# An encoder block on one core: output projection, queries, keys and memory output computed by rows, with the norms' results turned through DRAM

## The chip, the cores and the metric

The kernel runs on one core of a Trainium2 chip. The metric is the device time of one execution in microseconds; the time of a kernel is the median of its runs. The profile shows one execution in detail. Its engines are PE (TensorE matmul), PEld (TensorE weight load), DVE (VectorE), ACT (ScalarE), POOL (GpSimd) and SP (SyncE).

## The reference

One layer of an encoder for 256 tokens of width 2048, all in float32. Cut to what matters:

```python
h = rms_norm(x, norm_g[0])
q, k, v, g, lr, u_f, u_h, u_s = split(h @ w_in)
y_a = gla_mixer(q, k, v, g, lr, ...)                       # gated linear attention
y_b = rms_norm(fnet_mixer(u_f), grp_norm_g[0])             # fft over 256 tokens and 4 groups of 128 channels, real part
y_c = rms_norm(hyena_mixer(u_h, ...), grp_norm_g[1])       # long convolutions
y_d = rms_norm(shortconv_mixer(u_s, ...), grp_norm_g[2])
x = x + concat([y_a, y_b, y_c, y_d]) @ w_out               # output projection, 2048 x 2048
x = x + cross_attention(rms_norm(x, norm_g[1]), rms_norm(mem, mem_norm_g), w_xq, w_xkv, w_xo)
x = x + swiglu(rms_norm(x, norm_g[2]), w_gate_up, w_down)  # 2048 x 11264, 5632 x 2048
return rms_norm(x, final_norm_g)
```

Cross-attention has 4 heads of 512 over 256 memory tokens; `w_xq` gives the queries, `w_xkv` keys and values, and `w_xo` projects the heads' outputs back ("memory output").

## The kernel before, in words

**Numbers.** Every large product is taken in three parts: each float32 operand is split into a high half `h` (ACT copies it to float32r) and a low rest `l` (DVE subtracts), and the product is `hh + hl + lh`. An operand slot is a tile of 128 x 512: the high halves of 256 tokens, then their low halves.

**Weights.** The host packs all weights in the order in which they are used, in slabs of 128 x 2048 (1 MB, sixteen blocks of 128 x 128). `Stream._half` (L77) loads a slab through SP's queue, and for each half of it (eight blocks) ACT casts `wh` (L104) and DVE subtracts `wl` (L105). `Stream.take` (L109) hands out the next blocks and keeps up to three halves made ahead. Four halves are live until w_xo is nearly done, then three.

**Two forms of product.** By columns (`mm`, L304, called by `gemm`, L323): the weight block stays in the array and the activations stream. Per block there are two matmuls, `wh` against all 512 columns of the slot (L311) and `wl` against the 256 high ones (L312). The result is a block of 128 features x 256 tokens in two halves, which `merge` (L316) adds: ACT copies one out of PSUM, DVE adds. With `narrow` the first matmul is cut in two of 256 (L308, L309) that add up in PSUM, and no merge is needed. By rows (`gemm_rows`, L361, with `part_rows`, L353): the activations of 128 tokens stay and four weight blocks stream as 512 columns. For each half of the tokens there are three matmuls of 512 (L356, L357, L358). The result is 128 tokens x 512 features.

**Order of the work.** In `mixers` (L425): keys by columns (the first eight column blocks side by side, since memory's slots arrive one after the other), values by rows, then `w_in` in the order hyena, GLA's v by rows, GLA's q and k, three blocks of the short convolution, FNet narrow, the rest of the short convolution, GLA's gate. `out_proj` (L598) multiplies the four mixers' results, the first four column blocks in three parts, each behind one mixer. `attention` (L615) computes the queries of a head by columns, and each head's scores, softmax and values beside the next head's queries. `gate_up` (L757) and `down` (L834) work by rows.

**Between the products.** After w_out and w_xo a block of 128 features x 256 tokens is merged, added to the residual `x` (kept turned, features on partitions, in `res`), scaled by the norm's gain and split into the slots of the next product (`residual`, L584, and `rest`, L592). Squares are summed over features in `acc`, and a matmul by a column of ones (`rstd_begin`, L237, L247) gives the sum for each token. The norm's factor for each token is applied later, to the results. `rstd_end` (L291) spreads a factor over the partitions by a matmul with a diagonal matrix. `turn` (L813) takes the residual back to rows during gate_up: DVE transposes 32 x 32 pieces (L820), POOL stores them to DRAM (L823) and loads rows (L827). The hidden layer takes the same way: transposed by DVE (L776), stored (L779), loaded (L791) and split.

**Background work.** Everything small is a generator. `Background.poll` (called in every step of a product) advances those that are due by a clock that counts PE's and DVE's time as the author estimates it, and `drain` runs one to its end where its result is needed. The order in which the instructions then stand on each engine is laid out by the framework, which can put a later matmul ahead of one whose operands it takes to be late; `keep_place` (L219) holds some at their place.

Of the kernel before, what the change touches and what calls it, by code (L numbers as in the profile page):

```python
# [38 lines left out]
ROWS = ((256, 512), (704, 768), (NBLK - 48 * FT, NBLK))  # L39
# [86 lines left out]
class Background:  # L126
# [9 lines left out]
    def add(self, g):  # L136
        self.q.append([g, self.now])
        return g
# [29 lines left out]
class Block:  # L168
# [49 lines left out]

    def keep_place(self, mark):  # L219

        ins = self.nc.cur_bb.bb.instructions
        for n in range(mark, len(ins)):
            for j in range(n - 1, -1, -1):
                if ins[j].engine == ins[n].engine:
                    self.tc.add_manual_dep(ins[n], ins[j].name, mybir.DependencyInfo(
                        mybir.DependencyClass.NoSync, mybir.DependencyReason.DATA), reason="order")
                    break

    def sumsq(self, acc, src, first):
        if first:  # L230
            self.nc.scalar.activation(acc, src, AF.Square)
        else:
            s = self.tmp()
            self.nc.scalar.activation(s, src, AF.Square)
            self.tt(acc, acc, s, ALU.add)
# [33 lines left out]
    def rstd_bank(self, y, g=0, whole=False):  # L269

        nc = self.nc
        if whole:
            dg = self.dgp.tile([P, R], F32R, name="dgh", tag="dgh", bufs=2).bitcast(F32)
            self.bg.dve(256, 2)
            for r in range(2):
                s = slice(r * P, (r + 1) * P)
                nc.vector.tensor_scalar(out=dg[:, s], in0=self.ident, scalar1=y[:, 2 * g + r:2 * g + r + 1], scalar2=None, op0=ALU.mult)
            p = self.bank()
            nc.tensor.matmul(p[:, 0:R], self.ones, dg, start=True, stop=True)
            return p[:, 0:R]  # L280
# [5 lines left out]
        p = self.bank()  # L286
        for d in dg:
            nc.tensor.matmul(p[:, 0:R], self.onesr, d, start=d is dg[0], stop=d is dg[1])
        return p[:, 0:R]

    def rstd_end(self, y, g=0, keep=None, whole=False):  # L291
        rs = keep.tile([P, R], F32, name=f"krs{next(self.kept)}") if keep else self.rp.tile([P, R], F32, name="rs", tag="rs")
        self.nc.scalar.copy(rs, self.rstd_bank(y, g, whole))
        return rs

    def rstd_later(self, acc, n, box, keep=None, wait=2):

        box["col"] = self.rstd_begin([[acc]], n, keep)
        for _ in range(wait):
            yield  # L300
        box["rs"] = self.rstd_end(box["col"], 0, keep)
# [51 lines left out]
    def part_rows(self, p, r, slot, wh, wl, start, stop):  # L353

        hi, lo = slot[:, r * P:(r + 1) * P], slot[:, R + r * P:R + (r + 1) * P]
        self.nc.tensor.matmul(p[:, :], hi, wh, start=start, stop=False)  # L356
        self.nc.tensor.matmul(p[:, :], hi, wl, start=False, stop=False)  # L357
        self.nc.tensor.matmul(p[:, :], lo, wh, start=False, stop=stop)  # L358
        self.bg.pe(0.687)

    def gemm_rows(self, w, cols, slots, done=None, parts=None, before=None):  # L361
# [3 lines left out]
        nk = len(slots)  # L365
        for part, ks in enumerate(parts or [range(nk)]):
            if before:
                before(part)
            for k in ks:
                for p, col in zip(ps, cols):  # L370
                    wh, wl = self.st.take(w, k, col, 4)
                    for r in range(2):
                        self.part_rows(p[r], r, slots[k], wh, wl, k == 0, k == nk - 1)
                if done:
                    done(k)
                self.bg.poll()
        return ps


    def run(self):  # L380
# [9 lines left out]
        self.acc = cp.tile([P, R], F32, name="acc")  # L390
        self.mg = cp.tile([P, 16], F32, name="mg")
        self.eps = cp.tile([P, 8], F32, name="eps")[:, 0:1]
        self.gap(cp, 224)

        self.kd = nc.dram_tensor("keys", (P, 16 * R), F32, kind="Internal").ap()
        self.xr = nc.dram_tensor("xrows", (R, D), F32, kind="Internal").ap()
# [18 lines left out]
        make_identity(nc, self.ident)  # L415
        with self.tc.tile_pool(name="wx", bufs=1) as st.extra:
# [8 lines left out]
    def mixers(self):  # L425
# [42 lines left out]
        def prepare(mid):  # L468
# [5 lines left out]
            self.rsm = self.rstd_end(self.rcm, 0, self.cp)  # L474
            self.bg.add(hy.filters())
            nc.sync.dma_start(gl.lrw, self.t["lrw"])
            yield from squares("x", c[1])
            col = self.rstd_cols(c[1][:, 0:2], D)

            while not rows:  # L480
                yield SOON
            self.rsx = self.rstd_end(col, 0, mid, True)

        UF, UH, US = 1568, 2080, 3616
        cols, cur = [], {}
        for j in range(4):
            cols += [US + 512 + j * P, US + 1024 + j * P, US + j * P]
# [15 lines left out]
        with tc.tile_pool(name="mid", bufs=1) as mid:  # L503
            self.dgp = mid
            gl = Gla(self, mid)
            with tc.tile_pool(name="hyp", bufs=1) as hyp, tc.tile_pool(name="k2", bufs=8) as k2:
# [6 lines left out]
                def ev_k(i, p):  # L513
                    if i == 8:
                        for k in range(0, KT, 4):
                            self.load_x(k, 4)
                    nc.gpsimd.dma_start(self.kd[:, i * R:(i + 1) * R], self.merge(p))

                self.gemm("w_xkv", [i * P for i in range(16)], h, ev_k, first=(8, [[k] for k in range(KT)]), before=start_m)
                for hd in range(4):  # L520
                    for r, p in enumerate(self.gemm_rows("w_xkv", [D + hd * 512], h, start_x if hd == 3 else rows.append)[0]):
                        for c in range(2):
                            v, o = self.tmp(), (2 * hd + r) * 512 + c * R
                            nc.scalar.activation(v, p[:, c * R:(c + 1) * R], AF.Copy, scale=self.rcm[:, r:r + 1])
                            nc.gpsimd.dma_start(self.vd[:, o:o + R], v)
                self.bg.drain()
# [10 lines left out]
                self.gemm("w_in", cols[0:NSC], h, ev_s, narrow=True)  # L537
                self.bg.drain()

            with tc.tile_pool(name="glp", bufs=1) as glp:  # L540
                gl.open(glp)
                fn = Fnet(self, glp)
# [918 lines left out]
```

## Time and profile before

| | |
|---|---|
| time, median of 3 runs | 1484.07 us (1484.03 to 1484.11) |
| the profiled execution | 1483.97 us, its span 1482.2 us |
| mean granted clock of TensorE | 0.998 |
| DVE, ACT, POOL busy | 64%, 52%, 10% |
| DMA, mean share of 16 engines' time of the weights' queue | 53.9% |
| read from HBM | 291.18 MB, 206 GB/s with what is written |

Stages in the trace, by the start of their first large matmul, in us of the span:

| stage | from | to |
|---|---|---|
| keys | 5 | 98 |
| values | 98 | 195 |
| w_in | 195 | 461 |
| w_out | 461 | 550 |
| w_xq (attention beside it) | 550 | 658 |
| w_xo | 658 | 754 |
| w_gate_up | 754 | 1234 |
| w_down | 1234 | 1482 |

How to read a row of a profile: "L311 PE MATMUL pg<-act,wh 128*128 128x512 f32 x1" is line 311, engine, operation, the tile written and those read, the shape, and the count; times are in us unless marked ns. In a table of groups the numbers behind the bar are the busy time in us, the mean ns of one instruction, and the idle time of the engine ahead of them with what ended it. In a timeline the first two numbers are start and duration. Matmuls overlap: one of 512 columns is busy for 0.39 us, while the next starts 0.23 us after it.

### The profile page before, as it was taken

The page shows a single profiled execution, that of the slowest core. Times are in us where ns is not written, and L with a number is a line of the kernel's source. Part 1 is how long each engine was busy: PE and PEld are TensorE (multiplying, and loading weights), DVE is VectorE, ACT ScalarE, POOL GpSimd, SP SyncE. Part 2 cuts the span into 40 slices and gives each one's busy share as a digit, 9 for nine tenths or more (in the row PEclk, how much of TensorE's full clock was granted, in tenths as well). Part 3 has the DMA queues.
Part 4 walks back from the last instruction along what each step waited for, and adds up shares of the span by engine and source line. Part 5 has one row for each costly group of instructions (what it writes and reads, how often), then busy time and mean ns, then how long its engine had stood idle before and what let it go on. Part 6 is the DMA issues. An engine that isn't in the chain of part 4 may idle for free.

```text
span 1482.2 us, 19837 instructions
## 1 busy us (share of the span) xinstructions
PE 1471.8 (99%) x7586; PEld 1254.9 (85%) x7586; DVE 942.1 (64%) x1379; ACT 766.3 (52%) x1147; POOL 150.1 (10%) x260
## 2 busy tenths in 40 slices
PE   9999999999999999999999999999999999999997
PEld 8888888899899888888888888888888888888886
DVE  6687768778677777877665554555554456544444
ACT  6566655458555656656544444444444445434344
POOL 0100100000000001200042411111110112000000
PEclk9999999999999999999999999999999999999999
DMA  9976554454446555544567756666666666555554
GB/s 359 353 250 209 203 195 162 169 184 144 167 155 220 196 188 199 197 166 160 184 198 252 242 210 215 220 222 227 211 207 212 222 224 228 186 191 194 199 198 143
DMA packets 56174, 306.11 MB, mean 207 GB/s; under 512 B 9197, under 2 KB 10510, under 8 KB 24464
## 3 DMA queue, kind: packets, MB, share of 16 engines
q1 hardware_dynamic: 45632, 281.11, 53.9%
q0 software_dynamic: 10016, 23.08, 4.9%
q8 instruction: 59, 0.97, 0.3%
q10 hardware_dynamic: 432, 0.66, 0.1%
q14 instruction: 35, 0.29, 0.1%
HBM read 291.18 MB, written 13.63 MB: 206 GB/s over the span
## 4 chain that ended last, share of the span: by engine, by line
PE 96%; ACT 1%; DVE 1%; issue 0%; DMA 0%; SPq 0%; ACTq 0%; DVEq 0%
PE pg L311 21%; PE pg L356 17%; PE pg L357 17%; PE pg L358 17%; PE pg L312 11%; PE pm L357 1%; PE pm L356 1%; PE pm L358 1%; PE pm L311 1%; PE pm L986 1%; PE pg L308 1%; PE pg L309 1%; PE pm L738 1%; PE pm L312 1%; PE pm L711 0%; ACT wh L104 0%
## 5 line engine op out<-in xcount | busy, mean ns | idle before, releaser
L105 DVE TENSOR_TENSOR wl<-raw,wh 128x1024 fp32r<-128x1024 f32 (+1 forms) x503 | 611.7, 1218 | 469.9 <-ACT wh L104 464.7
L104 ACT CAST wh<-raw 128x1024 fp32r<-128x1024 f32 (+1 forms) x503 | 523.7, 1042 | 577.9 <-PE pg L358 391.6
L311 PE MATMUL pg<-act,wh 128*128 128x512 f32 x1296 | 455.9, 394 | 0.2 <-DVE act L196 0.2
L312 PE MATMUL pg<-act,wl 128*128 128x256 f32 x1472 | 412.1, 280 | 0.0
L356 PE MATMUL pg<-wh,act 128*128 128x512 f32 x1008 | 393.1, 390 | 0.0
L358 PE MATMUL pg<-wh,act 128*128 128x512 f32 x1008 | 392.4, 389 | 0.0
L357 PE MATMUL pg<-wl,act 128*128 128x512 f32 x1008 | 392.3, 389 | 0.0
L311 PEld LDWEIGHTS pg<-act,wh 128*128 128x128 f32 x1296 | 243.3, 188 | 53.4 <-DVE act L196 0.5
L312 PEld LDWEIGHTS pg<-act,wl 128*128 128x128 f32 x1472 | 276.8, 188 | 1.1 <-issue 0.4
L356 PEld LDWEIGHTS pg<-wh,act 128*128 128x128 f32 x1008 | 189.2, 188 | 40.2 <-issue 0.4
L358 PEld LDWEIGHTS pg<-wh,act 128*128 128x128 f32 x1008 | 189.2, 188 | 39.8
L357 PEld LDWEIGHTS pg<-wl,act 128*128 128x128 f32 x1008 | 189.3, 188 | 39.1
L779 POOL DMA_DIRECT2D hidden<-u x88 | 57.1, 656 | 311.0 <-DVE u L776 309.5
L308 PE MATMUL pg<-act,wh 128*128 128x256 f32 x176 | 50.0, 284 | 0.0
L309 PE MATMUL pg<-act,wh 128*128 128x256 f32 x176 | 49.5, 281 | 0.0
L356 PE MATMUL pg<-wh,f 128*128 128x512 f32 x120 | 46.7, 389 | 0.0
L357 PE MATMUL pg<-wl,f 128*128 128x512 f32 x120 | 46.7, 389 | 0.0
L358 PE MATMUL pg<-wh,f 128*128 128x512 f32 x120 | 46.7, 389 | 0.0
L196 DVE TENSOR_TENSOR tmp<-pg,tmp 128x256 f32<-128x256 f32 x86 | 35.9, 418 | 8.5 <-ACT tmp L318 6.9
L823 POOL DMA_DIRECT2D xrows<-tmp x48 | 27.7, 586 | 129.1 <-DVE tmp L820 126.0
L318 ACT COPY tmp<-pg 128x256 f32<-128x256 f32 x85 | 31.0, 366 | 9.5 <-PE pg L312 8.7
L308 PEld LDWEIGHTS pg<-act,wh 128*128 128x128 f32 x176 | 33.3, 189 | 0.1
(285 smaller groups left out, 1252.8 us busy)
## 6 DMA issues: line engine op xcount, KB each, us to landing
raw<-in_W SPq DMA_DIRECT2D x246, 1024.0 KB, 4.9
raw<-in_W SPq DMA_DIRECT2D x11, 512.0 KB, 7.4
hidden<-u POOLq DMA_DIRECT2D x88, 64.0 KB, 3.1
tmp<-hidden POOLq DMA_DIRECT2D x44, 128.0 KB, 4.2
res<-in_xT SPq DMA_DIRECT2D x8, 512.0 KB, 6.0
k<-in_mem SPq DMA_DIRECT2D x8, 256.0 KB, 7.9
k<-in_x SPq DMA_DIRECT2D x8, 256.0 KB, 8.3
keys<-tmp POOLq DMA_DIRECT2D x16, 128.0 KB, 5.9
```

The lines of the kernel that those rows point to most:

```text
L104: nc.scalar.copy(wh[:, a:b], r[:, a:b])
L105: nc.vector.tensor_tensor(out=wl[:, a:b], in0=r[:, a:b], in1=wh[:, a:b].bitcast(F32), op=ALU.subtract)
L196: self.nc.vector.tensor_tensor(out=out, in0=a, in1=b, op=op)
L308: self.nc.tensor.matmul(p[:, 0:R], wh, slot[:, 0:R], start=start, stop=False)
L309: self.nc.tensor.matmul(p[:, 0:R], wh, slot[:, R:512], start=False, stop=False)
L311: self.nc.tensor.matmul(p[:, :], wh, slot[:, :], start=start, stop=False)
L312: self.nc.tensor.matmul(p[:, 0:R], wl, slot[:, 0:R], start=False, stop=stop)
L318: self.nc.scalar.copy(t, p[:, R:512])
L356: self.nc.tensor.matmul(p[:, :], hi, wh, start=start, stop=False)
L357: self.nc.tensor.matmul(p[:, :], hi, wl, start=False, stop=False)
L358: self.nc.tensor.matmul(p[:, :], lo, wh, start=False, stop=stop)
L779: nc.gpsimd.dma_start(to[:, :, 32 * a:32 * a + 32], u[32 * a:32 * a + 32, :].rearrange("f (b t) -> f b t", t=32))
```

## The change

- **By rows.** Keys (in groups of two, one and one of 512 columns), output projection, queries and memory output (two, one, one) and FNet's projection go from `gemm` to `gemm_rows`. The order of the packed weights follows (`ROWS` marks which halves lie at the rows' offset).
- **Residual by rows.** `x` is loaded by rows; a result of 128 tokens x 512 features is added to it as it is (`add_rows`), and its squares are summed by ACT along the row (`sq`, then `row_norm`). `acc`, its column sums by matmul and `turn` go.
- **Turned through DRAM.** What the next product needs with features on partitions (the scaled, split residual after w_out and w_xo, and the queries) is transposed by DVE in pieces of 32 x 32, stored by POOL in runs of 32 elements (`store_turned`, `turned`) and loaded back in tiles of 128 x 256 (`arrive`), which ACT and DVE split. For each block of 512 columns that is 4 transposes, 16 stores and 4 loads. Keys are stored in the same way.
- **Order of w_out.** Its first two column blocks run together, in the order hyena, GLA, short convolution, FNet (before: four column blocks of 128, hyena and short convolution, FNet, GLA).
- **FNet.** Projection by rows; the transform over tokens comes first, on sums and differences of the two halves of the tokens, then the one over channels; both in split halves (before: over channels first, in plain float32).
- **Norms' factors.** `rstd_end` becomes two steps with a pause between them; one in plain float32 (`whole`, L279) is now in split halves too. The squares of x are taken once the first values are under way.
- **Last column block.** The residual's columns 1536 to 2047 enter the last product's PSUM bank by four matmuls with the identity at the start of gate_up (before: eight transposes at the start of down).

The diff, cut to its core:

```diff
-ROWS = ((256, 512), (704, 768), (NBLK - 48 * FT, NBLK))
+ROWS = ((0, 512), (704, 768), (880, 944), (1152, NBLK))
...
+    def store_turned(self, to, u, src):
+        nc = self.nc
+        self.bg.dve(src.shape[1])
+        nc.vector.transpose(u, src)
+        to = to.rearrange("(b f) t -> f b t", f=32)
+        for a in range(4):
+            nc.gpsimd.dma_start(to[:, :, 32 * a:32 * a + 32],
+                                u[32 * a:32 * a + 32, :].rearrange("f (b t) -> f b t", t=32))
...
-                self.gemm("w_xkv", [i * P for i in range(16)], h, ev_k, first=(8, [[k] for k in range(KT)]), before=start_m)
+                for cols in ([0, 512], [1024], [1536]):
+                    first = dict(parts=[[k] for k in range(KT)], before=start_m) if len(cols) > 1 else {}
+                    for c, ps in zip(cols, self.gemm_rows("w_xkv", cols, h, **first)):
+                        for r in range(2):
+                            self.store_turned(self.kd[c:c + 512, r * P:(r + 1) * P], hy.piece(), ps[r][:, :])
...
-                self.gemm("w_in", [UF + i * P for i in range(4)], h, lambda i, p: nc.scalar.copy(fn.u[i], p[:, 0:R]), narrow=True)
+                fn.feed(self.gemm_rows("w_in", [UF], h)[0])
...
-                self.out_proj(lambda n: self.bg.drain((g_sc, g_fn, g_gla)[n]))
+                self.out_proj(lambda n: self.bg.drain((g_gla, g_sc, g_fn)[n]))
...
+    def turned(self, to, c, srcs):
+        for r, x in enumerate(srcs):
+            for j in range(0, 512, R):
+                self.store_turned(to[c * 512 + j:c * 512 + j + R, r * P:(r + 1) * P], self.tmp(), x[:, j:j + R])
+
+    def arrive(self, src, c, put, ok=None):
+        m = []
+        for k in range(4 * c, 4 * c + 4):
+            m.append(self.tmp())
+            self.nc.gpsimd.dma_start(m[-1], src[k * P:(k + 1) * P, :])
+        yield 9.0
+        while ok and not ok():
             yield SOON
+        for i, t in enumerate(m):
+            mark = self.mark()
+            put(4 * c + i, t)
+            self.keep_place(mark)
+            yield SOON
+
+    def add_rows(self, n, c, ps):
+        for r in range(2):
+            x = self.half(c, r)
+            self.tt(x, x, ps[r], ALU.add)
+        for r in range(2):
+            self.nc.scalar.activation(self.bank()[:, :], self.half(c, r), AF.Square, accum_out=self.sq[n][:, 4 * r + c:4 * r + c + 1])
+        self.turned(self.xf[n], c, [self.half(c, r) for r in range(2)])
...
-        self.gemm("w_out", [i * P for i in range(16)], slots,
-                  lambda i, p: self.residual(i, p, V_NG + 16 + i, h2[i] if i < 8 else None),
-                  first=(4, [list(range(8, 16)), list(range(4, 8)), list(range(0, 4))]), before=ready)
-        self.late = self.bg.add(self.rest(h2, 8, V_NG + 16))
+        put = lambda k, t: self.split_scaled(h2[k], t, self.gvec(V_NG + 16, k))
+        free = self.st.n + 192 + 32
+        def done(c, ps):
+            self.add_rows(0, c, ps)
+            self.late.append(self.bg.add(self.arrive(self.xf[0], c, put, c > 1 and (lambda: self.st.n >= free)), go=True))
+        for c, ps in enumerate(self.gemm_rows("w_out", [0, 512], slots, parts=[range(k, k + 4) for k in (8, 0, 12, 4)], before=ready)):
+            done(c, ps)
+        for c, ks in ((2, [range(16)]), (3, [range(8, 16), range(8)])):
+            done(c, self.gemm_rows("w_out", [c * 512], slots, parts=ks)[0])
...
             for hd in range(4):
-                q = []
-                if hd > 1:
-                    self.bg.drain(gens[hd - 2], True)
-                self.gemm("w_xq", [(4 * hd + i) * P for i in range(4)], self.h2, lambda i, p: ev_q(q, p), first=(4, lp),
-                          before=lambda n: n and hd == 0 and self.bg.drain(self.late))
-                gens.append(self.bg.add(scores(hd, q)))
+                first = dict(parts=[range(8), range(8, 12), range(12, 16)],
+                             before=lambda n: [self.bg.drain(g) for g in late[:n + 2]]) if hd == 0 else {}
+                self.turned(self.qf, hd, self.gemm_rows("w_xq", [hd * 512], self.h2, **first)[0])
+                self.bg.add(scores(hd), go=True)
...
-            self.gemm("w_xo", [i * P for i in range(16)], o,
-                      ev_o,
-                      first=(4, [list(range(12)), list(range(12, 16))]), before=lambda n: n == 1 and self.bg.drain())
-            self.late = self.bg.add(self.rest(h3, 12, V_NG + 32))
+            for c, ps in enumerate(self.gemm_rows("w_xo", [0, 512], o, parts=[range(12), range(12, 16)],
+                                                  before=lambda n: n and self.bg.drain())):
+                done(c, ps)
+            for c in (2, 3):
+                done(c, self.gemm_rows("w_xo", [c * 512], o)[0])
+                st.extra = None
...
 class Fnet:
+        def triple(p, left, right, start, stop):
+            for n, (i, j) in enumerate(((0, 0), (0, 1), (1, 0))):
+                nc.tensor.matmul(p, left[i], right[j], start=start and n == 0, stop=stop and n == 2)
```

## The prediction

> **What bounds the kernel now.** I read the page first: its busy times, then its chain.
>
> ```profile
> PE 1471.8 (99%) x7586; PEld 1254.9 (85%) x7586; DVE 942.1 (64%) x1379; ACT 766.3 (52%) x1147; POOL 150.1 (10%) x260
> ...
> PE 96%; ACT 1%; DVE 1%; issue 0%; DMA 0%; SPq 0%; ACTq 0%; DVEq 0%
> ```
>
> PE is busy for all but 10 us, and the chain that ended last is PE for 96%. The table of PE's waits says how little it waits for others:
>
> ```profile
> PE pm L409 <- DVE eps L410: 1.1, 1, 1.1
> PE pm L1028 <- ACT tmp L980: 0.3, 1, 0.3
> PE pm L312 <- DVE wl L105: 0.2, 1, 0.2
> PE pm L311 <- ACT wh L104: 0.2, 1, 0.2
> PE pg L311 <- DVE act L196: 0.2, 1, 0.2
> ```
>
> The time is therefore the sum of PE's steps, start to start; only a matmul saved, a cheaper one, or a new wait of PE counts. A busy PE isn't PE at its peak, so I next read start times in stretches without a wait, from the timeline of PE. In w_out by columns (a pair L311, L312 for each block of weights, 128x128):
>
> ```profile
> 485.80 0.39 PE L311 MATMUL pg<-act,wh 128*128 128x512 f32 x1
> 486.03 0.28 PE L312 MATMUL pg<-act,wl 128*128 128x256 f32 x1
> ...
> 517.69 0.39 PE L311 MATMUL pg<-act,wh 128*128 128x512 f32 x1
> ```
>
> From the first L311 to the last are 92 blocks in 31.89 us: 346.6 ns a block. In w_gate_up by rows:
>
> ```profile
> 899.83 0.39 PE L358 MATMUL pg<-wh,act 128*128 128x512 f32 x1
> 900.05 0.39 PE L356 MATMUL pg<-wh,act 128*128 128x512 f32 x1
> ...
> 939.95 0.39 PE L358 MATMUL pg<-wh,act 128*128 128x512 f32 x1
> ```
>
> 177 matmuls in 40.12 us: 226.7 ns each. Six of them (three for each half of the tokens) serve four blocks, so a block costs 340.0 ns. The third form, narrow (three matmuls of 256 a block), in w_in:
>
> ```profile
> 329.13 0.28 PE L308 MATMUL pg<-act,wh 128*128 128x256 f32 x1
> ...
> 334.95 0.28 PE L309 MATMUL pg<-act,wh 128*128 128x256 f32 x1
> ```
>
> 49 matmuls in 5.82 us: 118.8 ns each, 356.4 ns a block.
>
> **The change part by part.** 1. *Output projection, queries, keys, memory output by rows.* Each has 16 x 16 blocks, 1024 together: 1024 x (346.6 - 340.0) = **-6.8 us**. The first four blocks, cut into halves of 256, cost under 0.1 us more.
>
> The Trainium skill, "TensorE: Matmul & The Clock Gate", section "Back-to-back issue gap", gives a lone warm matmul N/2.4 + 2.5 ns: by it the forms would cost 325.0 and 323.7 ns, and part 1 would give 1.3 us. The trace has 226.7 ns where the rule has 215.8, so here each matmul carries a larger fixed share, and rows save half a matmul a block; I go by the trace.
>
> 2. *FNet's projection by rows*: 64 blocks, 64 x (356.4 - 340.0) = **-1.0 us**.
>
> 3. *FNet's transforms* are taken in split halves. PE's timeline of before:
>
> ```profile
> 364.78 1.89 PE L1346 MATMUL pm<-fc,fu 128*128 128x256 f32 x8
> ...
> 367.91 2.27 PE L1346 MATMUL pm<-fc,fu 128*128 128x256 f32 x8
> ...
> 372.10 1.95 PE L1356 MATMUL pm<-fc,fa 128*128 128x128 f32 x16
> ...
> 376.67 1.95 PE L1356 MATMUL pm<-fc,fa 128*128 128x128 f32 x16
> ```
>
> 8.06 us, less four tails of 0.16 us that lie under the next matmul (0.39 busy against 0.23 start to start): 7.4. After: 24 of 256 (x 118.8 ns) and 12 of 512 (x 226.7) are 5.6. **-1.8 us**. If the moving operand read in two pieces costs 227 instead of 119 ns for 24 matmuls, +2.6; nearest row: no cost.
>
> 4. *Norms.* By form, PE's groups that go or change:
>
> ```profile
> L869 PE MATMUL pm<-ident,res 128*128 128x128 f32 x8 | 1.2, 272 | 0.0
> L247 PE MATMUL pm<-ones,acc 128*128 128x1 f32 x8 | 1.1, 242 | 0.0
> ...
> L279 PE MATMUL pm<-dgh,ones 128*128 128x256 f32 x2 | 0.6, 380 | 0.0
> ```
>
> L247's column sums of `acc` go: at most -1.1; I take -0.8 for overlapping tails. L279 (0.6 busy, about 0.4 start to start) becomes two of 118.8 ns: -0.2. L869's eight (about 0.9 start to start) become four of 226.7: 0. **-1.0 us**. DVE and ACT lose 64 merges, the 32 pieces of sums and squares and the turn after w_xo; both are off the path, so that is worth nothing. Keys' stores at the start stand 450 us ahead of their readers: nothing. x's rows replace xT in equal bytes on SP's queue, ahead of their sums by a part of w_out (10.9 us): nothing, and 1 us if they are late. The start itself is bound by the first loads: within 0.5 us.
>
> Parts 1 to 4: -6.8 - 1.0 - 1.8 - 1.0 = **-10.6 us**.
>
> 5. *New waits: the way through DRAM.* A block of 512 columns now leaves w_out, w_xq or w_xo by rows, is turned by DVE (4 transposes), stored by POOL in 16 DMAs of 32 KB, loaded in 4 of 128 KB, split by ACT and DVE, and only then multiplied. Before holds the same stores and loads, in POOL's timeline:
>
> ```profile
> 757.66 7.52 POOL L823 DMA_DIRECT2D xrows<-tmp  x13 [121.28 <-DVE tmp L820]
> 766.47 7.48 POOL L823 DMA_DIRECT2D xrows<-tmp  x13 [1.28 <-DMA xrows<-tmp]
> 774.91 3.47 POOL L823 DMA_DIRECT2D xrows<-tmp  x6 [0.96 <-issue]
> 778.36 1.14 POOL L827 DMA_DIRECT2D res<-xrows  x2
> 782.71 1.09 POOL L827 DMA_DIRECT2D res<-xrows  x2 [3.21 <-DMA xrows<-tmp]
> ```
>
> 0.58 us a store, and a load waits 3 to 4 us for the last store. Landings, from the table of DMAs, and DVE's groups:
>
> ```profile
> tmp<-hidden POOLq DMA_DIRECT2D x44, 128.0 KB, 4.2
> ...
> xrows<-tmp POOLq DMA_DIRECT2D x48, 32.0 KB, 3.8
> ```
> ```profile
> L105 DVE TENSOR_TENSOR wl<-raw,wh 128x1024 fp32r<-128x1024 f32 x498 | 609.0, 1224 | 467.3 <-ACT wh L104 462.1 <-PE pg L312 2.6 <-ACT tmp L318 1.2
> ...
> L200 DVE SCALAR_TENSOR_TENSOR act<-res,vec,act 128x256 fp32r<-128x256 f32 x32 | 15.1, 478 | 0.0
> ...
> L820 DVE STREAM_TRANSPOSE tmp<-res 128x256 f32<-128x256 f32 x12 | 4.8, 427 | 0.0
> ...
> L196 DVE TENSOR_TENSOR res<-res,pg 128x512 f32<-128x512 f32 x6 | 3.8, 679 | 0.0
> ```
>
> A round trip from the first transpose: 0.4; 12 stores until the first tile's data are out, 7.0; landing 3.8; load 0.6 + 4.2; split about 0.9: the first tile after 17 us, the last after about 20. Where a block is used, by the changed kernel's own order of instructions priced as above:
>
> - Last block of w_out, read by w_xq's first block at k = 12. PE is given 24 triples of that block and then 9 of the next ahead of it: 33 x 0.68 = 22.4 us. On DVE, between w_out's end and the first transpose, stand two sums (1.4), two splits of weights (2.4), the norm's ten small operations (1.6) and two scaled splits (1.0): 6.4. First tile at 6.4 + 17 = 23: a wait of 0 to 2 us, the last tile at 26 against 26.5. POOL's stores of this block stand behind the loads of the one before; nobody else waits on POOL there.
> - Queries of head 0: 15.9 us until their first matmul, 19.7 until the last; the trip needs 17 and 20: 0 to 1.5 us. Head 1: 26.4, but its transposes stand on DVE behind head 0's softmax (some 7 us): 0 to 1. Heads 2 and 3: 23.6 and 23.0: 0.
> - Last block of w_xo, read by w_gate_up at k = 12: 24 steps x 1.36 = 32.7 us against 26: 0.
>
> Together 0 to 4.5 us new. Against that stand 0.2 us at L311 <- act in w_out, and attention's small gaps, which change places. Below nothing: at most the 2 us of waits in the table. I take **+1.6 us**, the middle.
>
> Sum: -10.6 + 1.6 = -9.0. The profiled execution took 1483.97 us (span 1482.2 and 1.8 around it), 0.1 under the median of the runs, 1484.07: 1483.97 - 9.0 = **1475.0 us**.
>
> **The rivals.**
>
> *A. The gaps close.* The order of PE is laid out anew around each handoff, and what waited in before no longer does; the new trips arrive in time. -10.6 - 2 = -12.6: 1471.4. For it: PE's next steps are put ahead of late ones. Against: only 2 us are there to win.
>
> *B. Only part of a trip is hidden.* Each trip takes 1 to 4 us more than summed; three of them (w_out's last block, heads 0 and 1) have next to no spare. 3 x 1 to 3 x 4 on top of -9.0: 1478 to 1487. For it: landings above are medians, and half are longer; against: before's 32 stores and loads ran beside the same stream of weights.
>
> *C. Slower: the trips outlast their cover.* One mechanism: stores in runs of 128 bytes and their loads, landing beside the weights' stream. The longest landings in the trace, of the loads of kv:
>
> ```profile
> DMA to landing us min/median/max: 2.3/4.3/9.5
> ```
>
> 9.5 us at most against 4.2 taken, so +5 us a trip is possible; each of the three then makes PE wait that much: 3 x 5 = 15, -9.0 + 15 = +6, 1490. It decides from 3.7 us a trip (11.2 us) on; below that the change still gains. Against: the median landing is 3.8 and 4.2, and 32 such stores went through in one stretch above.
> The Trainium skill, "DMA: Bandwidth & Descriptors", section "Specifications", puts the least transfer for full rate at 512 bytes, below which a DMA reads, modifies and writes. The trace has the 128-byte stores at 3.8 us a landing, which is in the trip already.
>
> *D. Rows save less than the trace's stretches say.* The gap between the forms may belong to the stage and not to the form: if a matmul cost its columns plus a fixed 2.5 ns, part 1 would give 1.3 in place of 6.8 us: 1480.5. Both stretches ran at a full granted clock without a wait, which speaks against it. (The figure is that of the rule above.)
>
> **How the numbers follow.** Forecast (PE's sum holds, new waits 0 to 4.5 us): 0.66, 1473 to 1478. A: 0.10, 1470.5 to 1473. B: 0.13. C: 0.06. D: 0.05. The range takes the forecast, A and D and the unknown costs (split moving operand +2.6, late x +1, start 0.5): **1470.5 to 1481**, with 0.66 + 0.10 + 0.05 and a third of B, 0.85, in it; above it lies the rest of B, and C. A measurement here tells apart about 0.2%, 3 us. Faster by more than that (under 1481.1): those same cases, 0.85. Within it: the rest of B, 0.09. Slower: C, 0.06.
>
> **What would show it.** PE's groups: the column pairs fall from 1424 blocks to 400, the rows' triples rise from 1216 to 1762, each still 389 ns busy and 227 start to start, in w_out and w_xq too. FNet's transforms: under 6 us in all. PE's waits: no line over 2.5 us; the longest ones at w_xq's k = 12 and at the first scores. A wait of PE for a split `act` or `q` that stands behind a DMA, of 4 us or more, says B or C; triples at more than 230 ns say D. Wrong would be the whole if PE's total of waits rose over 10 us.

## The result, and the profile after

The changed kernel takes **1491.9 us** (median of 13 runs, 1485.8 to 1493.4); the kernel before took 1484.3 us beside it (13 runs, 1484.0 to 1487.8). The ratio is 1.004, with a 95% interval of 1.0028 to 1.0052: slower by about 7.6 us, where 1475.0 us was forecast and 1470.5 to 1481.0 given as the range. The profiled execution took 1486.86 us (span 1485.1), near the low end of the runs.

The page of the changed kernel, busy times and chain:

```profile
PE 1465.4 (99%) x6960; PEld 1223.4 (82%) x6960; DVE 925.7 (62%) x1324; ACT 751.9 (51%) x1092; POOL 269.1 (18%) x463
...
PE 88%; DMA 5%; POOL 2%; DVE 2%; issue 1%; ACT 1%; SPq 0%; POOLq 0%; DVEq 0%; ACTq 0%
```

PE has 626 matmuls fewer and is 6.4 us less busy, and yet the span is 2.9 us longer. The chain says why: PE's share fell from 96% to 88%, and DMA, POOL and DVE have come in. PE's waits, all of them (us in total, times, longest):

```profile
PE pm L765 <- ACT q L208: 3.6, 2, 2.7
PE pg L347 <- ACT act L212: 3.1, 1, 3.1
PE pm L784 <- DVE tmp L778: 1.9, 2, 1.3
PE pm L416 <- DVE eps L417: 1.1, 1, 1.1
PE pm L766 <- DVE q L200: 1.0, 1, 1.0
PE pg L348 <- DVE wl L105: 0.6, 1, 0.6
```

Before there were 2 us in all. But for L416, all of it is new, and waits for something that came through DRAM (`act` of w_out's last block, `q` of the heads), or for softmax and weights queued behind it. By the start of each stage's first matmul, in us; the second profile, the run without trips and that with wide stores are told below:

| | before | after | after, second profile | without trips | wide stores |
|---|---|---|---|---|---|
| start of w_out | 460.7 | 455.4 | 455.4 | 454.9 | 456.4 |
| w_out | 89.2 | 88.5 | 88.4 | 88.4 | 88.5 |
| w_xq and w_xo | 203.9 | **212.9** | **215.6** | 199.3 | 202.4 |
| w_gate_up to the last matmul | 720.1 | 720.1 | 719.7 | 719.2 | 719.2 |
| profiled execution | 1483.97 | 1486.86 | 1489.04 | 1471.83 | 1476.36 |

So the change does win 5.3 us up to w_out and 0.7 in it; it loses 9 us and more in attention, where 3 to 4 us of gain were due. The first wait, in PE's timeline of the changed kernel:

```profile
565.64 0.39 PE L347 MATMUL pg<-wh,act 128*128 128x512 f32 x1
569.13 0.50 PE L347 MATMUL pg<-wh,act 128*128 128x512 f32 x1 [3.10 <-ACT act L212]
...
570.61 0.63 PE L349 MATMUL pg<-wh,act 128*128 128x512 f32 x1
571.04 0.63 PE L347 MATMUL pg<-wh,act 128*128 128x512 f32 x1
571.47 0.63 PE L348 MATMUL pg<-wl,act 128*128 128x512 f32 x1
571.89 0.63 PE L347 MATMUL pg<-wh,act 128*128 128x512 f32 x1
...
574.10 0.40 PE L347 MATMUL pg<-wh,act 128*128 128x512 f32 x1
```

PE stood for 3.1 us, and behind it the matmuls come every 427 ns instead of 227, for 3.4 us. The table by stretches has PE's granted clock in the column behind the engines (1.00 is full speed):

```profile
569.00:571.00 2.00, 1.87 (x6) 1.41 (x7) 1.43 (x2) 2.00 (x5) 0.00 (x0) 0.81 0.00 0
571.00:573.60 2.60, 2.60 (x8) 1.99 (x6) 2.60 (x8) 1.44 (x5) 0.50 (x1) 0.50 0.00 0
573.60:590.00 16.40, 16.40 (x73) 13.31 (x72) 10.50 (x16) 7.83 (x11) 10.93 (x20) 1.00 0.76 257
```

The clock is halved after the wait, and full again at 573.6. By start times (565.64 to 574.10) this wait costs 3.3 us and another 1.8 behind it, not 3.3 alone. And the chain shows that there is not one trip ahead of it but one behind the other:

```profile
545.70 4.18 DMA tmp<-features
549.91 0.52 ACT act L212
...
550.86 0.45 DVE tmp L377
551.59 1.35 POOL features L380 x3
...
557.95 4.17 DMA features<-tmp
...
562.69 5.86 DMA tmp<-features
568.57 0.52 ACT act L212
569.13 0.50 PE pg L347
```

The last block's transposes (550.86) stand on DVE behind the scaled splits of the block before, which wait for that block's landing (549.9). They start 7.0 us after w_xq's first matmul (543.9), where 6.4 was summed. POOL's side of it:

```profile
545.13 1.14 POOL L612 DMA_DIRECT2D tmp<-features  x2 [1.87 <-DMA features<-tmp]
549.57 1.09 POOL L612 DMA_DIRECT2D tmp<-features  x2 [3.30 <-DMA features<-tmp]
551.59 9.25 POOL L380 DMA_DIRECT2D features<-tmp  x16 [0.93 <-DVE tmp L377]
562.69 1.14 POOL L612 DMA_DIRECT2D tmp<-features  x2 [1.86 <-DMA features<-tmp]
```

Sixteen stores take 9.25 us, one after the other, and each pair of loads makes POOL wait in line for a store's landing. Of the 17.7 us from the first transpose to the landing (550.86 to 568.55), POOL's stores up to the one waited for take 6.4 (551.59 to 557.95), the two landings in the chain 4.2 and 5.9. So a POOL that is busy for 18% of the span is the longest single part of this handoff, and the load took 5.86 us from its issue where 0.6 + 4.2 was summed.

### The profile page after: what moved, and what is told of

Same layout as the page of the kernel before. It is cut to its first block, busy times and chain, and to the rows that moved or that the text cites. A ratio compares the mean times of both kernels' runs of the same rounds, so it can differ in the third digit from the quotient of the medians.

```text
span 1485.1 us, 18747 instructions
## 1 busy us (share of the span) xinstructions
PE 1465.4 (99%) x6960; PEld 1223.4 (82%) x6960; DVE 925.7 (62%) x1324; ACT 751.9 (51%) x1092; POOL 269.1 (18%) x463
## 4 chain that ended last, share of the span: by engine, by line
PE 88%; DMA 5%; POOL 2%; DVE 2%; issue 1%; ACT 1%; SPq 0%; POOLq 0%; DVEq 0%; ACTq 0%
PE pg L348 23%; PE pg L349 23%; PE pg L347 23%; PE pg L298 6%; PE pg L299 4%; DMA features<-tmp 1%; PE pm L349 1%; PE pm L348 1%; PE pm L347 1%; DMA queries<-tmp 1%; PE pm L1010 1%; DMA tmp<-features 1%; POOL features L380 1%; DMA tmp<-queries 1%; PE pg L295 1%
## 5 line engine op out<-in xcount | busy, mean ns | idle before, releaser
L347 PE MATMUL pg<-wh,act 128*128 128x512 f32 (+1 forms) x1522 | 594.1, 391 | 3.1 <-ACT act L212 3.1
L348 PE MATMUL pg<-wl,act 128*128 128x512 f32 (+1 forms) x1522 | 593.7, 390 | 0.8 <-DVE wl L105 0.6
L349 PE MATMUL pg<-wh,act 128*128 128x512 f32 (+1 forms) x1522 | 592.7, 390 | 0.0
L347 PEld LDWEIGHTS pg<-wh,act 128*128 128x128 f32 x1522 | 286.4, 188 | 64.4 <-ACT act L212 3.5
L348 PEld LDWEIGHTS pg<-wl,act 128*128 128x128 f32 x1522 | 286.5, 188 | 61.2 <-DVE wl L105 2.7
L349 PEld LDWEIGHTS pg<-wh,act 128*128 128x128 f32 x1522 | 286.4, 188 | 59.9 <-DVE act L204 0.2
L299 PE MATMUL pg<-act,wl 128*128 128x256 f32 x512 | 143.5, 280 | 0.0
L298 PE MATMUL pg<-act,wh 128*128 128x512 f32 x400 | 141.2, 395 | 0.0
L299 PEld LDWEIGHTS pg<-act,wl 128*128 128x128 f32 x512 | 96.3, 188 | 0.3
L298 PEld LDWEIGHTS pg<-act,wh 128*128 128x128 f32 x400 | 75.2, 188 | 16.2
L380 POOL DMA_DIRECT2D features<-tmp x128 | 74.1, 587 | 79.2 <-DVE tmp L377 70.8
L295 PE MATMUL pg<-act,wh 128*128 128x256 f32 x112 | 31.7, 283 | 0.0
```

What stands on the lines that cost most here:

```text
L295: self.nc.tensor.matmul(p[:, 0:R], wh, slot[:, 0:R], start=start, stop=False)
L298: self.nc.tensor.matmul(p[:, :], wh, slot[:, :], start=start, stop=False)
L299: self.nc.tensor.matmul(p[:, 0:R], wl, slot[:, 0:R], start=False, stop=stop)
L347: self.nc.tensor.matmul(p, hi, wh, start=start, stop=False)
L348: self.nc.tensor.matmul(p, hi, wl, start=False, stop=False)
L349: self.nc.tensor.matmul(p, lo, wh, start=False, stop=stop)
```

## The experiments

Theory T: what goes through DRAM comes late, and PE's waits for it (with the half clock behind them) are the whole loss. Rival R: rows are not cheaper, or 202 more DMAs slow the stream of weights.

**1. The changed kernel again, for a second profile.**

> The changed kernel unaltered, for a second profile: its runs spread from 1485.8 to 1493.4 us, and the one profiled so far was at the low end (1486.9). Theory T (PE waits for what is turned through DRAM): in a longer execution the extra time lies between w_out's end and w_gate_up's start and nowhere else, as longer waits for act and q behind DMAs and as matmuls at half the granted clock behind such waits; that stretch took 212.9 us in the first profile (203.9 before), and takes 212.9 plus whatever this execution is longer. Rival R (more DMAs and stores slow the stream of weights, or rows are slower per block): the extra time is spread over the stages, or stands at waits for wh and wl. An execution at 1492 would need 218 us there by T.

Measured: 1489.0 us. Up to w_out's end nothing differs by more than 0.1 us (table above); w_xq and w_xo took 2.7 us longer, which is more than the whole difference of 2.2. The extra time lies where T wants it. PE's waits for `wl` and `wh` grew too, from 0.6 to 2.0 us, which R also names; 0.7 of that stands at the kernel's start, and 1.1 at 558 and 562 us, behind splits for which ACT waited. It is number 2 that decides. The wait for w_out's last block was 3.4 us and followed by eleven matmuls at 427 ns. Here the last load landed 2.63 us after its issue, but the transposes stood 3.9 us later than in the first profile, behind the landing of the block before:

```profile
552.49 0.51 ACT L212 ACTIVATE act<-tmp,vec 128x256 fp32r<-128x256 f32 x1 [4.67 <-DMA tmp<-features]
554.74 1.42 DVE L377 STREAM_TRANSPOSE tmp<-res 128x256 f32<-128x256 f32 x4
```

**2. Without the trips' waits.**

```diff
-            self.late.append(self.bg.add(self.arrive(self.xf[0], c, put, ...), go=True))
+            self.late.append(self.bg.add(self.arrive(self.kd, c, put, ...), go=True)) 
...
-                yield from self.arrive(self.qf, hd, put, lambda: len(heads) > hd - 2)
+                yield from self.arrive(self.kd, hd, put, lambda: len(heads) > hd - 2)
```

The edit does the same to w_xo's blocks. The next products get the keys in place of the turned results, by loads that are issued ahead of the stores.

> Left out: what w_out, w_xq and w_xo give to the next product. The loads that fetch the turned blocks read the keys' tensor, written 400 us earlier, and are issued ahead of the stores, so nobody waits for a landing; all transposes, stores, loads, splits and matmuls stay. T: the waits behind the round trips go (about 10 us of waits and 2 us of half clock in the profile of 1486.9, more in longer executions): 1473 to 1477 us, about 16 us under the changed kernel, and the spread of its runs shrinks to under 2 us. R (weights slowed by 202 more DMAs, or rows not cheaper): stays at 1484 or more, with the spread.

Measured: **1472.2 us** (1471.8 to 1473.5), ratio to before 0.9918 (0.9904 to 0.9931). All of PE's waits:

```profile
PE pm L416 <- DVE eps L417: 1.1, 1, 1.1
PE pg L348 <- DVE wl L105: 0.2, 1, 0.2
```

All stores, loads, splits and matmuls are still there; only nobody waits for a landing. The trips cost 1491.9 - 1472.2 = 19.7 us in the medians, and with them goes the spread (1.7 us over 4 runs). R falls. 1472.2 is also what the rest of the change is worth: 12 us.

**3. The heads' part alone.** As 2, for the queries only.

> Left out: the queries that the heads use are those of another tensor (the keys'), loaded ahead of the queries' stores; the residual's blocks still go through DRAM. T: only the wait for w_out's last block stays (3.3 us and 2 us of half clock behind it in the profile of 1486.9): 1478 to 1484 us. If the heads' trips matter little and w_out's last block makes all of the loss: 1486 to 1492. R: as the changed kernel, 1486 to 1493.

Measured: 1484.9 us (1481.3 to 1488.3), ratio 1.0001 (0.9992 to 1.001). Of the 19.7 us the queries' trips have 7.0, and by difference those of w_out and w_xo 12.7. The upper end was missed by a little: in this profile PE waits for weights too.

```profile
PE pg L348 <- DVE wl L105: 4.2, 4, 2.3
PE pg L347 <- ACT act L212: 3.4, 1, 3.4
```

The first line is the second way in which a late landing costs: a split that waits on ACT or DVE for its data holds back the weights' casts behind it. At w_xo's end ACT stood 3.16 us for a landing, with the next two casts behind it (747.5 us), and PE waited 2.3 us for `wl` (until 750.1).

**4. Turned by PE.** w_out's last block and all queries.

```diff
+                    self.nc.tensor.transpose(p[:, j * R + r * P:j * R + (r + 1) * P],
+                                             srcs[2 * r + i // 2][:, j * P:(j + 1) * P], self.ident)
```

> Same results by another way: the last block of w_out and the queries of all four heads are turned by PE (8 transposes of 128x128 a block, 40 in all) and never go to DRAM; w_out's first three blocks and w_xo's four still do. T: 40 transposes at about 0.12 us are 5 us on PE, and the round trips that PE waited for are gone: 1477 to 1482 us, spread under 2 us, faster than before. R: no better than the changed kernel, 1486 to 1497.

Measured: 1481.2 us (1479.6 to 1482.5), ratio 0.9977 (0.9967 to 0.9987), faster than before. The 40 transposes stand in groups of two to four, mostly 109 ns apart. The waits for `act` and `q` are gone; 2.5 us for `wl` are left, 2.2 of them at w_xo's end.

**5. Filling the wait with matmuls.**

```diff
+                    for i in range(FILL):      # FILL = 16
+                        nc.tensor.matmul(p[:, :], self.h2[0][:, 0:P], self.h2[0], start=i == 0, stop=i == FILL - 1)
```

> The changed kernel with 16 matmuls of 512 more (3.6 us, their result is read by nobody), which stand on PE between w_xq's k = 11 and the matmuls that wait for w_out's last block. In both profiles of the changed kernel that wait was 3.1 to 3.4 us and the ten matmuls behind it took 427 ns instead of 227. If the half clock comes from PE standing idle, the fill takes the place of the wait, no matmul behind it takes 427 ns there, and 2 us are won: 1488 to 1491 against the changed kernel's 1491.9. If the half clock has another cause, the ten slow matmuls stay, and the time stays or grows by up to 3.6 us: 1491 to 1495.

Measured: 1491.7 us (1490.8 to 1496.9; the profiled execution is the longest). **Inconclusive**: the framework put six triples less of the next block (4.1 us) ahead of the wait, so that the fill took the place of other cover. The wait was 4.4 us there, and twelve matmuls at 427 ns followed.

**6 and 7. Queries by columns, and later splits.** Number 6 has the queries in the form of before and w_out's last block turned by PE; 7 has `yield 16.0` in place of `yield 9.0` in `arrive` as well.

> The changed kernel with the queries by columns as before (no trip; 256 blocks at 346.6 instead of 340.0 ns, +1.7 us against rows), w_out's last block turned by PE (8 transposes, +0.9 us); keys, w_out, w_xo, FNet as in the changed kernel. T (the trips are the whole loss): 1472.2 of the run without trips + 1.7 + 0.9 = 1475, up to 1478 where weights are split late behind a split of ACT or DVE that waits for a landing at w_xo's end (2.1 us in the run with all turned by PE). R (rows in w_out and w_xo lose by themselves): 1480 or more.

> As the run with queries by columns, and the splits of what comes from DRAM are put 16 us instead of 9 behind the loads' issue in the order of ACT and DVE. Second half of T: a split that stands too early on ACT and DVE holds back the splits of weights behind it, which PE then waits for. If so, the waits for wl at w_xo's end (2.1 us in the run with all turned by PE) go: 1474 to 1476, and 1 to 3 us under the same without the longer pause. If that wait has another cause (late weights): no difference.

Measured: 1480.9 us (1479.1 to 1482.4), ratio 0.9975 (0.9964 to 0.9986), and 1480.0 us (1479.0 to 1482.0), ratio 0.9974 (0.9963 to 0.9984). Both missed their expectation by 3 to 4 us, number 6 lies in the range that was set down for R (1480 or more), and the pause gave nothing that can be told. Against R stands number 11, which also has w_out and w_xo by rows and takes 1476.2 us. In 6 PE waits 3.3 us for `wl`, most of it at w_xo's third block, with eight matmuls at half clock behind one wait of 1.9 us. In 7 ACT shows what holds the weights:

```profile
741.41 0.91 ACT L212 ACTIVATE act<-tmp,vec 128x256 fp32r<-128x256 f32 x2 [3.51 <-DMA tmp<-features]
```

The splits stood later, and their data came later still: w_xo's first two blocks end together, so POOL has 32 stores and 8 loads at once, and all behind them shift. That pointed to POOL.

**8. Keys and FNet alone**, on the kernel before.

> The kernel before with only those parts of the change that send nothing through DRAM on the way: keys and FNet's projection by rows, FNet's transforms in split halves, the norms' factors in two steps; w_out, queries, w_xo, residual and turn as before. Terms of the prediction: -1.7 (256 blocks of keys) -1.0 -1.8 -0.2 = -4.7: 1479 to 1480.5. The profile of the changed kernel has w_out start 5.3 us earlier than before, which would give 1479. If rows gain nothing over columns (prediction's D): 1481.5 to 1482.5.

Measured: 1485.6 us (1484.9 to 1487.1), ratio 1.0011 (1.0002 to 1.002): a miss. w_out starts at 455.5 as expected, but takes 96.2 us instead of 89.2, mostly for one reason:

```profile
PE pg L306 <- DVE act L200: 4.7, 1, 4.7
```

FNet's result is now late for its old place as w_out's second part, and four matmuls at half clock follow. The order of w_out in the change isn't a detail.

**9. The same, FNet's part last.**

```diff
-                  first=(4, [list(range(8, 16)), list(range(4, 8)), list(range(0, 4))]), before=ready)
+                  first=(4, [range(8, 12), range(12, 16), range(0, 4), range(4, 8)]), before=ready)
```

> As the run with keys and FNet alone (1485.6, where PE waited 4.7 us for FNet's result at w_out's second part, and w_out took 96.2 us instead of 89.2), but w_out takes its parts in the order hyena, short convolution, GLA, FNet, so that FNet's result is needed 5.5 us later. If that wait hid the gain: 1479 to 1481, as w_out starts 5.3 us earlier than before. If the loss came with the keys or FNet themselves: 1484 or more.

Measured: 1480.4 us (1479.8 to 1481.8), ratio 0.9973 (0.9961 to 0.9984): 4.0 us less than before, where the terms say 4.7.

**10. Half as many stores.**

```diff
-            for j in range(0, 512, R):
-                self.store_turned(to[c * 512 + j:c * 512 + j + R, r * P:(r + 1) * P], self.tmp(), x[:, j:j + R])
+            u = self.twp.tile([P, 512], F32, name="tw", tag="tw")
+            self.store_turned(to[c * 512:(c + 1) * 512, r * P:(r + 1) * P], u, x[:, 0:512])
```

> The changed kernel with the turned pieces 512 wide instead of 256: 8 stores of 64 KB a block of 512 columns instead of 16 of 32 KB, the same bytes in the same runs of 128. By the profile a 64 KB store of that shape holds POOL for 0.656 us and a 32 KB one for 0.584, so a block's stores take 5.2 us of POOL instead of 9.3. Theory P (the trip is long because POOL issues one DMA after the other and its loads wait in line for the stores ahead): each trip is 3 to 4 us shorter, the waits behind it (3.3 us and 2 us of half clock at w_out's end, 2.9, 1.4 and 1.1 us at scores, wl at w_xo's end) shrink or go: 1478 to 1485. Rival Q (the landings beside the weights' stream make it late; bytes and runs decide): 1488 to 1492.

Measured: **1476.1 us** (1475.4 to 1477.0), ratio 0.9945 (0.9932 to 0.9957): with number 11 the fastest of the kernels that leave nothing out, 8.4 us under before and 15.8 under the change, and 2 us under the range of theory P. POOL at w_out's last block:

```profile
546.78 0.65 POOL L381 DMA_DIRECT2D features<-tw  x1 [10.33 <-DVE tw L378]
547.55 2.22 POOL L613 DMA_DIRECT2D tmp<-features  x4
549.76 2.62 POOL L381 DMA_DIRECT2D features<-tw  x4
553.66 1.94 POOL L381 DMA_DIRECT2D features<-tw  x3 [1.28 <-DMA tmp<-features]
559.81 2.22 POOL L613 DMA_DIRECT2D tmp<-features  x4 [4.21 <-ACT wh L104]
```

The stores take 5.2 us instead of 9.3. The median landing of the residual's blocks is not shorter than in the changed kernel but longer (stores 4.7 against 3.9 us, loads 4.9 against 3.9; for the queries 3.7 against 4.3, and 4.0 in both). With the same bytes in the same runs 15.8 us are gone, so Q falls. But the trip from the first transpose to the landing isn't shorter either (545.8 to 563.7; in the changed kernel 550.9 to 568.6): the transposes start 0.9 us after w_xq's first matmul instead of 7.0. The edit had changed the buffers too, and the number alone doesn't show which of the two helped.

**11. Queries by columns, both last blocks turned by PE, wide stores.**

> Keys, w_out, w_xo and FNet by rows as in the changed kernel, queries by columns as before, stores 512 wide, and the last blocks of w_out and of w_xo turned by PE (16 transposes, 1.8 us). By T and P nothing that PE waits for goes through DRAM with little cover any more: the run without trips, 1472.2, + 1.7 (queries by columns) + 1.8 = 1475.7, up to 1478 with 2 us of weights split late at w_xo's end as in the run with queries by columns (1480.9). If the two stay as they were: 1480 to 1481.

Measured: 1476.2 us (1476.0 to 1476.7), ratio 0.9946 (0.9933 to 0.9958), as summed; no wait for anything from DRAM is left. It equals number 10.

**12 and 13. Buffers or stores?** Number 12 keeps the 16 narrow stores and has own buffers (`twp`, 4 of 128x256; `tp` 7 instead of 11), 13 changes one condition of the changed kernel, so that the third block's splits come behind the last block's transposes:

```diff
-... c > 1 and (lambda: self.st.n >= free)), go=True))
+... c > 1 and (lambda: self.st.n > free + (32 if c == 2 else 0))), go=True))
```

> The changed kernel with 16 stores of 32 KB a block as it had them, but the turned pieces lie in buffers of their own (4 of 128x256; the shared ring of small buffers goes from 11 to 7): what the run with wide stores changed beside the number of stores. By the trace of that run the trip from the first transpose to the landing did not get shorter (17.9 us at w_out's last block against 17.7), only the transposes stand right behind the sums on DVE (1.2 us after PE's end instead of 7.3). Theory S (in the changed kernel a block's transposes stand on DVE behind splits that wait for the landing of the block before, so one trip waits for the other, and the buffers decide that order): 1476 to 1481. Theory P (16 stores in series on POOL make the loss): 1486 to 1492.

> The changed kernel, buffers and stores as they are. Only the splits of w_out's third block of 512 columns are issued one step later, so that on DVE the transposes of the last block stand ahead of them instead of behind two of them. By S the wait for w_out's last block (3.1 to 4.4 us in three profiles, and 2 us of half clock behind each) shrinks by the time in which the transposes stood behind a landing (0.7 us in the fast profile, 4.5 in the longer one): 1487 to 1490, with less spread. By P nothing changes: 1491 to 1492.

Measured: 1483.6 us (1480.2 to 1488.5), ratio 0.9995 (0.9984 to 1.0005), and 1488.8 us (1485.4 to 1500.4), ratio 1.0035 (1.0017 to 1.0052). Number 12 lies between the ranges of S (the order on DVE) and P (POOL's line): neither theory has it alone. From 1491.9 the buffers give 8.3 us and half the stores another 7.5 (to 1476.1). Number 13 lies in S's range, but its interval overlaps that of the changed kernel (1.0028 to 1.0052), and its spread did not shrink as expected (1485.4 to 1500.4): that the order alone gains time isn't shown. POOL in number 12, where the transposes start right behind the sums (544.8):

```profile
545.52 0.61 POOL L381 DMA_DIRECT2D features<-tw  x1 [0.61 <-DVE tw L378]
549.29 1.10 POOL L613 DMA_DIRECT2D tmp<-features  x2 [3.15 <-DMA features<-tw]
550.38 4.64 POOL L381 DMA_DIRECT2D features<-tw  x8
556.56 0.58 POOL L381 DMA_DIRECT2D features<-tw  x1 [1.55 <-DMA features<-tw]
557.30 3.45 POOL L381 DMA_DIRECT2D features<-tw  x6 [0.16 <-issue]
563.40 1.13 POOL L613 DMA_DIRECT2D tmp<-features  x2 [2.65 <-DMA features<-tw]
```

The block has its transposes 6 us earlier than in the changed kernel, and yet its last store ends at 560.8 in both: with 16 stores and the block before in the same line, and with loads that stand in that line until a store has landed (3.15 and 2.65 us), POOL is the bound, and PE waits for it (number 12's waits):

```profile
PE pg L348 <- ACT act L213: 6.4, 1, 6.4
PE pm L766 <- ACT q L209: 2.3, 1, 2.3
```

With 8 stores POOL is through at 555.6. Number 13 cured the place that it changed, where 0.3 us of wait for `act` are left, but its longest wait is now at the first head: PE came there sooner (586.7 against 593.1 us), and the queries' trip was as long as ever.

```profile
PE pm L765 <- ACT q L208: 4.3, 2, 4.1
```

## Why the prediction was wrong

- **What bounds the kernel** (PE's steps; any new wait counts in full): right. The sign that it named for being wrong, PE's waits over 10 us in all, came true (11.3 by the table). The two longest stand where it put them, at w_xq's k = 12 and at the first scores.
- **Parts 1 to 4, -10.6 us**: right. Column pairs fell to 400 and row triples rose to 1762. In w_out 155 matmuls by rows (501.68 to 536.85) took 35.17 us, 226.9 ns each. FNet's transforms take 5.8 us (24 at 122 and 12 at 240 ns, start to start) against 5.6. The profile without trips is 12.1 us shorter than that of before, keys and FNet alone gain 4.0 us: rival D is out.
- **Part 5, "I take +1.6 us", is the step that failed.** Measured: 15 us in the profile (1486.9 - 1471.8), 19.7 in the medians. Of the 15, 13.6 lie in w_xq and w_xo: 9.6 are waits, 1.8 half clock, and the other 2.2 steps that are a little longer, most of them at the scores. The mechanism stood in the text, but four things in its sum were wrong.
  - *The spare was none, and the trip was a little longer.* For w_out's last block the cover was nearly right (22.4 us summed; PE came to it at 566.0, 22.1 us after w_xq's first matmul). The block was taken to be there after 23 us and came after 25.2, and after 27.3 in the second profile. Each microsecond above the sum went straight to the end.
  - *One handoff was summed as if it stood alone.* Two scaled splits were counted at 1.0 us ahead of the transposes; they wait for the landing of the block before (0.6 us more in the first profile, 4.5 in the second). POOL's line was noted ("behind the loads of the one before; nobody else waits on POOL there"), but it makes each trip wait for the last: heads 2 and 3, put at 0, and w_xo's end pay for that.
  - *A wait was priced at its length.* Seven times in these profiles PE stood for 3.1 us or more (3.1 to 6.4) behind w_out's start; each time 4 to 12 matmuls at 427 ns followed, which cost 1.5 to 2.9 us more. Of ten waits of 1.9 to 2.8 us, two were followed by such a stretch.
  - *A late split was not followed to the weights behind it* on ACT and DVE (`wl`: up to 4 us in number 3).
- **The rivals.** B (1478 to 1487) has the profiled execution, C (1490, given 0.06) the median. C's price was right, its mechanism only by half: it wanted longer landings, and their medians are as before (3.9 and 3.9 us against 3.8 and 4.2), though single ones on the path were longer (5.86 us in the first profile, 6.75 in the second, for the load of the block before). What took long throughout was the issue of 16 stores in a line with the loads. C's threshold was also mis-summed: from -9.0 the gain is gone at 3.0 us a trip, not at 3.7. That the three trips "have next to no spare" was written, and then the middle of 0 to 4.5 was taken: a sum with no spare errs to one side only.

The Trainium skill, "TensorE: Matmul & The Clock Gate", section "What's actually happening", says that the array's clock is halved after at least one idle window of about 3.4 us, and that these windows run freely. The trace agrees with half the clock (0.50), which lasted 3.4 us in the first profile and 6.8 in the second; it set in 1.1 us after the wait's end in the first and 2.1 us after its start in the second, which fits windows that run freely. But a wait of 3.1 us was enough here, and so were one of 1.9 and one of 2.3 us.

What stays open: the executions at 1491 us and more, 8 of 13, weren't caught in a profile (those caught took 1486.9 and 1489.0), so that where their last 3 to 5 us lie is inferred from the runs without trips, which don't have them. How much of number 12's gain is the order on DVE and how much the buffers themselves wasn't settled. Half clock was seen behind each of the seven waits of 3.1 us or more, but that idleness alone brings it isn't shown: the trial by a fill failed.

## What to carry to other kernels

Where PE is busy throughout, a cheaper form of product pays what its steps say, and a new handoff pays it back as soon as its trip is as long as its cover: demand spare, don't take the middle. Count a trip through DRAM by its DMAs in the queue that issues them, with the trips ahead of it in the same line and in DVE's order, and make it of few, large DMAs (here half the stores and own buffers turned +7.6 us into -8.4). The waits of PE of 3.1 us and more cost 1.5 to 2.9 us beyond what they lasted.

## What the runs showed of the hardware

- A DMA issue on POOL costs nearly the same for 32 KB (587 ns) and 64 KB (656 ns) in runs of 128 bytes, so at these sizes the number of DMAs sets the time.
- A round trip through DRAM for a block of 512 columns x 256 tokens takes 15 to 19 us from the first transpose to the first landing with 16 stores in the changed kernel; turning the block on PE takes eight steps, mostly of 109 ns.
- One wait of 3.1 us is enough to be followed by half of PE's granted clock for 3.4 us; of ten waits of 1.9 to 2.8 us two were followed so.
